# Attention in a two-layer streaming encoder: turned weights two blocks later, second exponentials left in PSUM, gates and loads cut up, sums of squares in one product

## The chip, the core and the metric

The kernel runs on one NeuronCore of a Trainium2 chip. The metric is the device time of one execution in microseconds (us). PE is the tensor engine (TensorE), DVE the vector engine (VectorE), ACT the scalar engine (ScalarE), POOL GpSimd, SP the queue that issues every DMA here.

## The reference, cut to the part that matters

Two layers of an encoder work on 1024 prompt tokens and 32 sample tokens. Branch B of each layer is differential attention: 8 heads, each with two maps of 64 dimensions, whose softmaxes are subtracted.

```python
def diff_attn_core(q, k, v, lam, mask):
    s = jnp.einsum('bhqmd,bhkmd->bhmqk', q, k).astype(jnp.float32) * (D_QK ** -0.5)
    if mask is not None:
        s = jnp.where(mask, s, -jnp.inf)
    a = jax.nn.softmax(s, axis=-1)
    a = a[:, :, 0] - lam * a[:, :, 1]
    return jnp.einsum('bhqk,bhkv->bhqv', a.astype(v.dtype), v)
...
    o_b = rmsnorm(o_b.transpose(0, 2, 1, 3), p['diff_norm_w']) * (1.0 - lam_init)
    o_b = (o_b * jax.nn.silu(z_b.reshape(B, T, H_B, DV_B))).reshape(B, T, W_B)
```

The prompt's mask is block-causal in chunks of 64 keys; a sample token sees 128 cached keys and the 32 new ones.

## The kernel before

Data are float32. The large products split a matrix into two float32r parts, high and low (`qh` and `ql`, `vh` and `vl`, `aT[..][0]` and `aT[..][1]`), so one of them is two or three matmuls; small ones are plain float32.

A layer has a stage of projections and of the other branch, then `attn` (L963), then the output projections. The order of PE's instructions in `attn` is written out by hand: the program's order is PE's order. On the other engines and on SP's queue a planner orders the instructions by its model of time. What stands under `urgent()` (L216) counts as 150 instructions earlier there.

`attn` walks over 8 heads and, in each, over nine query blocks: 8 (the samples, 32 rows) and 0 to 7 (128 rows each; block i sees (i + 1) * 128 keys). For a block, `soft` (L988) issues the scores of both maps into PSUM tiles `psc` (pool `pb`, two buffers of 1024 columns): blocks 8 and 0 to 3 put both maps into one buffer, blocks 4 to 7 take one buffer per map. DVE masks 64 columns (L1011, L1017) and takes the maxima `nm` (L1012, L1018), ACT takes the exponentials into two SBUF tiles `e` with their sums, and `combine` (L893) adds on DVE: `e[0] += c * e[1]`, with c from the sums.

After a block's scores PE runs filler (`pad`, L206): matmuls of other projections of the layer (tiles `pd`), as many as are due by the planner's prices `P_SOFT`, `P_KEY` and `P_LATE`; `share` spreads the filler over the heads so that `P_REST` is left. Then `flush` (L977) runs what is due, with filler after each:

- `turn` (L1024) transposes the block before's e on PE into `pta` (pool `pt`, two buffers of 512 columns), four key blocks to a tile; ACT casts them to the high part of `aT`, DVE subtracts for the low part. The aT tiles are taken when an even block is met (L1075), and POOL clears the part that the even query block never fills (L1077).
- `av` (L1037), after each odd block: 3 * nkb matmuls of 256 columns into `pav`.
- `attn_out` (L1102): ACT squares and copies `pav`; DVE adds the two halves of the squares (`sqb`), ACT casts the sum to float32r (`sqx`), DVE subtracts for its low part; the column sums follow two flushes later as float32r matmuls with ones (`pss`, L1120).
- `attn_row` (L1130), once per head: the norm's factors, transposed and stored to `rrow`.
- `gate_b` (L1180), in the same step: three groups of columns; for each, loads of z, o and the broadcast factors r, the product with r on POOL (L1191), the product with z on DVE (L1192), a store. All tiles come from a pool of four buffers.

Loads and casts of the heads stand together: `prep_q` (L927) for the second half of the queries after block 8, `prep_v` (L948) after block 0, `prep_k` (L912) of the next head after block 4, `prep_q` of its first half after block 5. Each issues its DMAs (into `raw`, two buffers) and at once the casts on DVE or ACT and the subtractions on POOL. The tiles `k0`, `k1` have two buffers, the q and v tiles one.

Of the kernel before, what the change touches and what calls it, by code (L numbers as in the profile page):

```python
# [20 lines left out]
TP = 1024  # L21
TS = 32
# [16 lines left out]
class Net:  # L39
    AHEAD = 150  # L40
    CUT = 26
    LATE, P_REST, P_START = 27, 23e3, 1e3
# [850 lines left out]
    def combine(s, pool, e, sums, rows, n):  # L893

        c = pool.tile([128, 1], F32, tag="cf", name="cf")
        s.nc.vector.reciprocal(c[:rows], sums[:rows, 1:2])
        s.stt(c[:rows], c[:rows], s.nlam[:rows], sums[:rows, 0:1], OP.mult, OP.mult)
        s.stt(e[0][:rows, 0:n], e[1][:rows, 0:n], c[:rows], e[0][:rows, 0:n], OP.mult, OP.add)
# [13 lines left out]
    def prep_k(s, l, pool, hd, ckt):  # L912

        raw = pool.tile([128, T], F32, tag="raw", name="kraw")
        s.ld.dma_start(out=raw, in_=s.kscr[l][2 * hd:2 * hd + 2].rearrange("m d t -> (m d) t"))
        K = []
# [10 lines left out]
    def prep_q(s, l, pool, hd, part):  # L927

        c0, w = (128, 640) if part == 0 else (0, 512)
        Q = []  # L930
        for m in range(2):
            hm = 2 * hd + m
            raw = pool.tile([128, T], F32, tag="raw", name="qraw")[:, 0:w]
            for u in range(2):
                r = slice(64 * u, 64 * u + 64)
                if part == 0:
                    s.ld.dma_start(out=raw[r, 0:TS], in_=s.qscr[l][hm, :, TP:T])
                s.ld.dma_start(out=raw[r, c0:w], in_=s.qscr[l][hm, :, part * 512:part * 512 + 512])
            if part == 0:
                s.nc.gpsimd.memset(raw[:, TS:128], 0.0)  # L940
            q = pool.tile([128, w], F32R, tag=f"q{part}{m}", name="qh")
            low = pool.tile([128, w], F32R, tag=f"ql{part}{m}", name="ql")
# [5 lines left out]
    def prep_v(s, l, pool, hd):  # L948
        vr = pool.tile([128, T], F32, tag="raw", name="vr")[:, 0:TP].rearrange("p (b f) -> p b f", b=8)
        s.ld.dma_start(out=vr, in_=s.io["v_prompt"][l, 0, hd].rearrange("(b t) f -> t b f", t=128))  # L950
        vh = pool.tile([128, 8, 128], F32R, tag="vh", name="vh")
# [11 lines left out]
    def attn(s, l, pool):  # L963
# [24 lines left out]
        def soft(hd, i, K, Q):  # L988
            rows, n, lo = (128, (i + 1) * 128, 0) if i < 8 else (TS, 160, 32)
            qc = 0 if i == 8 else (i + 1) * 128 if i < 4 else (i - 4) * 128  # L990
            e, sums = [pool.tile([128, 1024], F32, tag="e", name="e") for m in range(2)], s.s0[:, :, i, hd]
# [14 lines left out]
            else:  # L1006
                for m in range(2):
# [5 lines left out]
                    s.act(e[m][:, 0:n], p[:, 0:n], AF.Exp, bias=nm[:, m:m + 1], accum_out=sums[:, m:m + 1])  # L1013
            if pair:
# [44 lines left out]
        K, QA, turns = s.prep_k(l, pool, 0, ckt), s.prep_q(l, pool, 0, 0), []  # L1059
        s.pad(s.P_FIRST)  # L1060
        for hd in range(H):
# [4 lines left out]
            for i in (8, 0, 1, 2, 3, 4, 5, 6, 7):  # L1066
                with s.urgent():
                    e = soft(hd, i, K, QA if i in (8, 0, 1, 2, 3) else QB)
                pad(s.P_SOFT + s.P_KEY * (2 if i == 8 else i + 1) + (s.P_START if hd == 0 and i in (8, 0) else 0))
                flush(turns)  # L1070
                turns = []
                if i % 2 == 0 and i < 8:
                    j = i // 2
                    nkb = 2 * j + 2
                    aT = [[pool.tile([128, 4, 256], F32R, tag=f"aT{a}", name=f"aT{a}") for a in range(2)] for _ in range((nkb + 3) // 4)]  # L1075
# [21 lines left out]
        while late or turns:  # L1097
            s.pad(s.P_END)
            flush(turns)
            turns = []  # L1100

    def attn_out(s, l, pool, hd, po, t0, n):  # L1102
# [6 lines left out]
        if n > 128:  # L1109

            x = pool.tile([128, 256], F32R, tag="sqx", name="sqx")
            s.tt(sq[0:64], sq[0:64], sq[64:128], OP.add)
            s.cp(x[0:64], sq[0:64])
            s.tt(x[64:128], sq[0:64], x[0:64].bitcast(F32), OP.subtract)

        def rest():
            ps = s.pt.tile([128, 512], F32, tag="pt", name="pss")
            if n > 128:
                for c in range(2):
                    s.mm(ps[:, c * 2:c * 2 + 2], x[:, c * 128:c * 128 + 128], s.onesr)  # L1120
                c0 = t0 // 128
                s.cp(s.sso[:, c0:c0 + 2, hd], ps[:, 0:4:2])
# [5 lines left out]
        return (lambda: rest) if n > 128 else rest  # L1128

    def attn_row(s, l, pool, hd):  # L1130
# [8 lines left out]
        def rest():  # L1139
# [5 lines left out]
            if hd < H - 1:  # L1145
                s.gate_b(l, s.gbp, hd)
# [33 lines left out]
    def gate_b(s, l, pool, hd, groups=(0, 1, 2), act=None):  # L1180

        for g in groups:
            t0, n = GROUPS[g]
            z, o, r = (pool.tile([128, 384], F32, tag="eb" if act else "gb", name=nm) for nm in ("ez", "eo", "er"))
            s.ld.dma_start(out=z[:, :n], in_=s.zscr[l][1][hd][:, t0:t0 + n])
            s.ld.dma_start(out=o[:, :n], in_=s.obscr[l][hd][:, t0:t0 + n])
            c0, cn = t0 // 128, min(n, TP - t0) // 128
            s.ld.dma_start(out=r[:, 0:cn * 128].rearrange("p (c t) -> p c t", t=128), in_=s.rrow[l][hd][c0:c0 + cn].partition_broadcast(128))
            if g == 2:
                s.ld.dma_start(out=r[:, 256:n], in_=s.rrow[l][hd][8, 0:TS].partition_broadcast(128))  # L1190
            s.tt(o[:, :n], o[:, :n], r[:, :n], OP.mult, eng=None if act else s.nc.gpsimd)  # L1191
            s.stt(o[:, :n], o[:, :n], s.dnw[:, l:l + 1], z[:, :n], OP.mult, OP.mult)  # L1192
            if act:
                s.split(act, hd, g, o, hd % 2)
            else:
                s.st.dma_start(out=s.obscr[l][hd][:, t0:t0 + n], in_=o[:, :n])
# [323 lines left out]
```

## Time and profile before

| | |
|---|---|
| median of 3 runs | 3691.12 us (3687.35 to 3693.28) |
| the profiled execution's own time | 3680.13 us |
| its span, first to last instruction | 3678.4 us |
| busy: PE, DVE, ACT, POOL | 3368.0, 2256.4, 1520.9, 1366.3 us |
| attention of layer 0 and of layer 1 | from about 1083 to 1680 us and from 2858 to 3450 us of the span |

"Busy" counts the time in which an engine executes at least one instruction. [...] A row of waits has the idle time of an engine in front of an instruction and the instruction that ended it; "pta L76 <- DVE aT L54" is a transposition that waited for DVE's subtraction. A matmul and its weight load (PEld) are two rows; a plain float32 product is two matmul instructions.

### The profile page before, as it was taken

How to read it: one execution, taken by the hardware profiler on the slowest of the kernel's cores; microseconds unless marked ns; L12 is line 12 of the kernel's file. 1: busy time of each engine (PE TensorE's matmuls, PEld its weight loads, DVE VectorE, ACT ScalarE, POOL GpSimd, SP SyncE). 2: the span in 40 equal slices, each digit the busy share in tenths (PEclk: the TensorE clock that was granted, in tenths of full speed). 3: DMA queues.
4: the chain of work that ended last, by engine and by line, in shares of the span. 5: the costliest groups of instructions: out<-in, count | busy, mean ns of one | idle time of the engine just before them, and what ended most of it. 6: DMA issues, size and time to landing. Idle time of an engine off the chain costs nothing. (4 is left out here: it accounts for less than half of the span.)

```text
span 3678.4 us, 58386 instructions
## 1 busy us (share of the span) xinstructions
PE 3368.0 (92%) x20752; PEld 3136.4 (85%) x20752; DVE 2256.4 (61%) x3810; ACT 1520.9 (41%) x4246; POOL 1366.3 (37%) x1259
## 2 busy tenths in 40 slices
PE   8988897899999989899999999879999999889999
PEld 6888897778988888899888888878898889878997
DVE  4676758851426667865447676787143566777554
ACT  4565552123534444443244656311254344444321
POOL 2455548811134343423012223792112444343310
PEclk9999999999999999999999999999999999999999
DMA  5454534266753444556433443424775434445644
GB/s 178 116 144 142 147 117 127 85 165 197 230 147 108 129 124 133 158 150 193 138 130 94 118 119 117 134 78 131 191 233 166 130 112 132 134 149 149 177 151 151
DMA packets 618987, 526.67 MB, mean 143 GB/s; under 512 B 107028, under 2 KB 567448, under 8 KB 618312
## 3 DMA queue, kind: packets, MB, share of 16 engines
q1 hardware_dynamic: 618696, 522.94, 48.3%
q8 instruction: 164, 2.69, 0.3%
q14 instruction: 127, 1.04, 0.1%
HBM read 342.49 MB, written 180.31 MB: 142 GB/s over the span
## 5 line engine op out<-in xcount | busy, mean ns | idle before, releaser
L72 PE MATMUL pd<-h,whi 128*128 128x384 f32 (+1 forms) x2688 | 707.9, 339 | 20.3 <-ACT u L69 13.2
L72 PE MATMUL pd<-mg,whi 128*128 128x384 f32 (+1 forms) x2688 | 698.1, 336 | 13.5 <-ACT u L69 11.7
L54 POOL TENSOR_TENSOR wlo<-wraw,whi 128x512 fp32r<-128x512 f32 (+1 forms) x220 | 432.7, 1976 | 494.6 <-ACT whi L69 444.0
L72 PEld LDWEIGHTS pd<-h,whi 128*128 128x128 f32 x2688 | 479.2, 195 | 29.8 <-ACT u L69 14.5
L72 PEld LDWEIGHTS pd<-mg,whi 128*128 128x128 f32 x2688 | 474.7, 193 | 22.1 <-ACT u L69 12.5
L72 PE MATMUL pd<-h,wlo 128*128 128x384 f32 (+1 forms) x1344 | 451.2, 336 | 0.0
L72 PE MATMUL pd<-mg,wlo 128*128 128x384 f32 (+1 forms) x1344 | 449.1, 334 | 0.0
L69 ACT CAST whi<-wraw 128x1024 fp32r<-128x1024 f32 (+1 forms) x304 | 259.1, 865 | 192.0 <-PE pd L72 61.7
L66 ACT ACTIVATE e<-psc,nm 32x160 f32<-32x160 f32 (+8 forms) x288 | 200.8, 700 | 307.3 <-DVE nm L1012 152.5
L72 PEld LDWEIGHTS pd<-h,wlo 128*128 128x128 f32 x1344 | 261.0, 194 | 2.3 <-issue 1.2
L72 PEld LDWEIGHTS pd<-mg,wlo 128*128 128x128 f32 x1344 | 259.0, 193 | 2.5 <-issue 1.2
L72 PE MATMUL ptok<-whi,mg 128*128 128x512 f32 x768 | 241.2, 395 | 5.2 <-DVE rt L54 3.4
L63 DVE SCALAR_TENSOR_TENSOR acc<-u,convT,acc 128x1059 f32<-128x1059 f32 x144 | 218.9, 1523 | 2.7
L72 PE MATMUL pr<-mg,whi 128*128 128x384 f32 (+1 forms) x768 | 196.2, 339 | 15.7 <-DVE rt L54 15.7
L72 PE MATMUL pr<-h,whi 128*128 128x384 f32 (+1 forms) x768 | 194.2, 338 | 15.3 <-DVE rt L54 15.2
L72 PE MATMUL pd<-oa,whi 128*128 128x384 f32 (+1 forms) x768 | 193.8, 330 | 5.2 <-DVE egt L63 3.7
L72 PE MATMUL pd<-ob,whi 128*128 128x384 f32 (+1 forms) x768 | 184.4, 326 | 5.7 <-ACT whi L69 2.0
L54 DVE TENSOR_TENSOR wlo<-wraw,whi 128x1024 fp32r<-128x1024 f32 x84 | 107.7, 1283 | 120.9 <-ACT whi L69 119.2
L72 PEld LDWEIGHTS ptok<-whi,mg 128*128 128x128 f32 x768 | 144.3, 189 | 37.3 <-DVE rt L54 3.6
L76 PE MATMUL pta<-ident,e 128*128 128x128 f32 (+1 forms) x608 | 98.4, 288 | 74.3 <-DVE aT L54 53.8
L54 DVE TENSOR_TENSOR itmp<-ub,X 128x624 f32<-128x624 f32 (+56 forms) x188 | 152.1, 809 | 15.1 <-DMA ub<-ublks 6.3
L72 PEld LDWEIGHTS pr<-mg,whi 128*128 128x128 f32 x768 | 140.2, 198 | 19.9 <-DVE rt L54 19.1
(319 smaller groups left out, 8043.1 us busy)
## 6 DMA issues: line engine op xcount, KB each, us to landing
wraw<-in_w_in SPq DMA_DIRECT2D x160, 512.0 KB
srec<-grec SPq DMA_DIRECT2D x128, 384.0 KB
grec<-rec SPq DMA_DIRECT2D x128, 192.0 KB
z<-zo SPq DMA_DIRECT2D x96, 192.0 KB
wraw<-in_w_ada SPq DMA_DIRECT2D x64, 256.0 KB
qraw<-qscr SPq DMA_DIRECT2D x128, 128.0 KB
egt<-z SPq DMA_DIRECT2D x64, 192.0 KB
eo<-ob SPq DMA_DIRECT2D x60, 192.0 KB
```

What stands on the lines that cost most here:

```text
L54: (eng or s.nc.vector).tensor_tensor(out, a, b, op=op)
L63: s.nc.vector.scalar_tensor_tensor(out, a, sc, b, op0=op0, op1=op1)
L66: s.nc.scalar.activation(out, a, func, **kw)
L69: s.nc.scalar.copy(out, a)
L72: s.nc.tensor.matmul(out, lhsT, rhs, start=start, stop=stop)
L76: s.nc.tensor.transpose(out, a, s.ident[0:n, 0:n])
```

## The change

- `combine` reads the second map's exponentials from PSUM: ACT writes them over the scores they come from. Only one `e` tile per block is taken. The combine is issued after the block's filler.
- `flush` runs the turns of the block before the last (`ready`), so a block is turned two blocks behind its scores. The aT tiles are taken in `turn`; POOL's clearing goes.
- In `av` the last key block is multiplied with the odd query block's 128 columns only, right after the first product.
- Loads and casts are separate functions; each load stands one or two blocks ahead of its casts, and the next head's first q half is cast after block 6.
- The sums of squares are plain float32 matmuls of `sq` with a column of ones, one flush earlier.
- The gates of a head are issued one group at a time, loads in one flush and use in the next; DVE's product with z comes first, POOL's with r second. Outside `attn` the same function serves the last head.
- `LATE`, the number of late steps that the filler's spread counts per head, is 29, not 27.

```diff
-    LATE, P_REST, P_START = 27, 23e3, 1e3
+    LATE, P_REST, P_START = 29, 23e3, 1e3
...
-        s.stt(e[0][:rows, 0:n], e[1][:rows, 0:n], c[:rows], e[0][:rows, 0:n], OP.mult, OP.add)
+        s.stt(e[0][:rows, 0:n], e[1], c[:rows], e[0][:rows, 0:n], OP.mult, OP.add)
...
-            e, sums = [pool.tile([128, 1024], F32, tag="e", name="e") for m in range(2)], s.s0[:, :, i, hd]
+            e, sums = [pool.tile([128, 1024], F32, tag="e", name="e"), None], s.s0[:, :, i, hd]
...
-                    s.act(e[m][:, 0:n], p[:, 0:n], AF.Exp, bias=nm[:, m:m + 1], accum_out=sums[:, m:m + 1])
+                    to = p if m else e[0]
+                    s.act(to[:, 0:n], p[:, 0:n], AF.Exp, bias=nm[:, m:m + 1], accum_out=sums[:, m:m + 1])
+                e[1] = p[:, 0:n]
...
-                for m in range(2):
-                    s.act(e[m][:rows, 0:n], pv[:rows, m, lo:lo + n], AF.Exp, bias=nm[:rows, m:m + 1], accum_out=sums[:rows, m:m + 1])
-            s.combine(pool, e, sums, rows, n)
-            return e[0]
+                e[1] = pv[:rows, 1, lo:lo + n]
+                for m, to in enumerate((e[0][:rows, 0:n], e[1])):
+                    s.act(to, pv[:rows, m, lo:lo + n], AF.Exp, bias=nm[:rows, m:m + 1], accum_out=sums[:rows, m:m + 1])
+            return e[0], lambda: s.combine(pool, e, sums, rows, n)
...
         def turn(hd, i, e, aT, v):
+            if i % 2 == 0:
+                aT[:] = [[pool.tile([128, 4, 256], F32R, tag=f"aT{a}", name=f"aT{a}") for a in range(2)] for _ in range((i + 5) // 4)]
...
-            s.accumulate(po[:, 0:256], [(v[:, kb], aT[kb // 4][a][:, kb % 4])
-                                        for kb in range(nkb) for v, a in ((vh, 0), (vl, 0), (vh, 1))])
+            order = [(0, 0)] + [(nkb - 1, x) for x in range(3)] + [(kb, x) for kb in range(nkb - 1) for x in range(3) if kb or x]
+            for k, (kb, x) in enumerate(order):
+                q0 = 128 if kb == nkb - 1 else 0
+                s.mm(po[:, q0:256], (vh, vl, vh)[x][:, kb], aT[kb // 4][x // 2][:, kb % 4, q0:256], start=k == 0, stop=k == len(order) - 1)
...
-                    e = soft(hd, i, K, QA if i in (8, 0, 1, 2, 3) else QB)
+                    e, comb = soft(hd, i, K, QA if i in (8, 0, 1, 2, 3) else QB)
                 pad(s.P_SOFT + s.P_KEY * (2 if i == 8 else i + 1) + (s.P_START if hd == 0 and i in (8, 0) else 0))
-                flush(turns)
-                turns = []
+                with s.urgent():
+                    comb()
+
+                flush(ready)
+                ready, turns = turns, []
                 if i % 2 == 0 and i < 8:
...
-                    for a in range(2):
-                        nc.gpsimd.memset(aT[(nkb - 1) // 4][a][:, (nkb - 1) % 4, 0:128].bitcast(F32), 0.0)
+                    aT = []
                 if i == 8:
                     turns.append(lambda hd=hd, e=e, vs=vs: sample(hd, e, vs))
-                    QB = s.prep_q(l, pool, hd, 1)
+                    raws = s.load_q(l, pool, hd, 1)
...
                 if i == 0:
-                    v.extend(s.prep_v(l, pool, hd))
+                    QB = s.prep_q(pool, raws, 1)
+                if i == 1:
+                    raws = s.load_v(l, pool, hd)
+                if i == 2:
+                    v.extend(s.prep_v(pool, raws))
                 if hd < H - 1:
...
+                    if i == 2:
+                        raws = s.load_k(l, pool, hd + 1)
                     if i == 4:
-                        Kn = s.prep_k(l, pool, hd + 1, ckt)
-                    if i == 5:
-                        QA = s.prep_q(l, pool, hd + 1, 0)
+                        Kn = s.prep_k(pool, raws, ckt)
+                        raws = s.load_q(l, pool, hd + 1, 0)
+                    if i == 6:
+                        QA = s.prep_q(pool, raws, 0)
...
-        while late or turns:
+        while late or turns or ready:
             s.pad(s.P_END)
-            flush(turns)
-            turns = []
+            flush(ready)
+            ready, turns = turns, []
...
-        if n > 128:
-
-            x = pool.tile([128, 256], F32R, tag="sqx", name="sqx")
-            s.tt(sq[0:64], sq[0:64], sq[64:128], OP.add)
-            s.cp(x[0:64], sq[0:64])
-            s.tt(x[64:128], sq[0:64], x[0:64].bitcast(F32), OP.subtract)
...
-                    s.mm(ps[:, c * 2:c * 2 + 2], x[:, c * 128:c * 128 + 128], s.onesr)
+                    s.mm(ps[:, c:c + 1], sq[:, c * 128:c * 128 + 128], s.ones[:, 0:1])
                 c0 = t0 // 128
-                s.cp(s.sso[:, c0:c0 + 2, hd], ps[:, 0:4:2])
+                s.cp(s.sso[:, c0:c0 + 2, hd], ps[:, 0:2])
...
-        return (lambda: rest) if n > 128 else rest
+        return rest
...
-                s.gate_b(l, s.gbp, hd)
+                return lambda: gate(0)
+
+        def gate(g):
+
+            x = s.gate_load(l, s.gbp, "gb", hd, g)
+
+            def use():
+                s.gate_use(l, hd, g, *x)
+                if g < 2:
+                    return lambda: gate(g + 1)
+            return use
...
+    def gate_use(s, l, hd, g, z, o, r, act=None):
+        t0, n = GROUPS[g]
+        s.stt(o[:, :n], o[:, :n], s.dnw[:, l:l + 1], z[:, :n], OP.mult, OP.mult)
+        s.tt(o[:, :n], o[:, :n], r[:, :n], OP.mult, eng=None if act else s.nc.gpsimd)
```

## Rows read from the trace of the kernel before

**Rows 1.** Windows of both attention stages: us, busy per engine, clock, DMA share, GB/s.
```profile
1083.00:1680.00 597.00, 545.59 (x3446) 519.95 (x3445) 407.79 (x742) 266.47 (x715) 242.57 (x216) 0.97 0.46 135
2858.00:3450.00 592.00, 540.63 (x3404) 514.64 (x3403) 406.36 (x736) 265.48 (x711) 238.42 (x214) 0.96 0.45 133
```

**Rows 2.** Windows of seven stretches at the low clock: their sum.
```profile
sum 47.60, PE 28.30 PEld 27.52 DVE 39.06 ACT 25.68 POOL 31.66; mean PE 4.04 PEld 3.93 DVE 5.58 ACT 3.67 POOL 4.52
```

**Rows 3.** PE's waits in both stages: us, times, longest us; layer 0, then 1.
```profile
PE pta L76 <- DVE aT L54: 25.4, 8, 6.3
PE psc L72 <- ACT e L66: 6.8, 5, 2.0
PE pta L76 <- DVE e L63: 3.7, 2, 1.9
...
PE pta L76 <- DVE aT L54: 28.5, 8, 6.8
PE pta L76 <- DVE e L63: 4.2, 2, 2.8
```

**Rows 4.** Timeline at a change of heads: start us, us, engine, what [idle <-releaser].
```profile
1228.99 1.44 DVE L920 CAST k<-kraw 64x1056 fp32r<-64x1056 f32 x2 [2.04 <-DMA kraw<-kscr]
1229.83 5.42 POOL L54 TENSOR_TENSOR k<-kraw,k 64x1056 fp32r<-64x1056 f32 x2 [4.88 <-DVE k L920]
1230.46 2.52 DVE L54 TENSOR_TENSOR sqb<-sqb 64x256 f32<-64x256 f32 x1
1233.01 0.40 ACT L69 CAST sqx<-sqb 64x256 fp32r<-64x256 f32 x1 [6.84 <-DVE sqb L54]
1233.45 2.09 DVE L54 TENSOR_TENSOR sqx<-sqb,sqx 64x256 fp32r<-64x256 f32 x1 [0.47 <-ACT sqx L69]
1235.57 1.16 DVE L54 TENSOR_TENSOR aT<-pta,aT 128x512 fp32r<-128x512 f32 x2
1236.31 0.90 PE L76 MATMUL pta<-ident,e 128*128 128x128 f32 x3 [6.30 <-DVE aT L54]
```

**Rows 5.** DVE's groups by shape, layer 0's attention: busy us, mean ns, idle before.
```profile
L54 DVE TENSOR_TENSOR sqx<-sqb,sqx 64x256 fp32r<-64x256 f32 x32 | 30.3, 946 | 4.5 <-ACT sqx L69 3.8
L54 DVE TENSOR_TENSOR sqb<-sqb 64x256 f32<-64x256 f32 x32 | 28.9, 902 | 22.4 <-ACT sqb L66 21.8
L63 DVE SCALAR_TENSOR_TENSOR zo<-zt,pd 128x384 f32<-128x384 f32 x16 | 8.7, 546 | 1.0 <-ACT zt L66 1.0
L63 DVE SCALAR_TENSOR_TENSOR e<-e,cf 128x384 f32<-128x384 f32 x8 | 4.9, 618 | 0.2
```

**Rows 6.** Timeline, PE: a float32 product, products of 256 columns, transposes.
```profile
1008.86 0.39 PE L72 MATMUL po<-w,srec 128*128 128x128 f32 x2
1204.83 0.28 PE L72 MATMUL pav<-aT,vh 128*128 128x256 f32 x1
1205.06 0.41 PE L72 MATMUL pav<-aT,vh 128*128 128x256 f32 x2
1214.12 0.82 PE L76 MATMUL pta<-ident,e 128*128 128x128 f32 x6
```

**Rows 7.** Timeline: block 6's combine and the next second map's scores; heads 1, 2.
```profile
1147.47 1.15 DVE L63 SCALAR_TENSOR_TENSOR e<-e,cf 128x896 f32<-128x896 f32 x1
1150.45 0.39 PE L72 MATMUL psc<-k,qh 128*128 128x512 f32 x1
1217.02 0.50 PE L72 MATMUL psc<-k,qh 128*128 128x512 f32 x1
1218.37 1.15 DVE L63 SCALAR_TENSOR_TENSOR e<-e,cf 128x896 f32<-128x896 f32 x1
```

**Rows 8.** DVE's waits in layer 0's attention.
```profile
DVE eo L63 <- POOL eo L54: 48.1, 20, 4.7
```

**Rows 9.** Windows of the second and third head of layer 0.
```profile
1160.40:1227.20 66.80, 64.12 (x421) 61.08 (x420) 42.67 (x81) 31.97 (x87) 27.10 (x26) 1.00 0.42 123
1227.20:1298.60 71.40, 65.06 (x416) 62.54 (x415) 45.30 (x83) 33.47 (x90) 30.36 (x27) 0.95 0.40 118
```

More of the change, by code (lines that the diff above doesn't have):

```diff
@@ L910, in attn_cache, with load_k, prep_k @@
         return ckt, rest
-    def prep_k(s, l, pool, hd, ckt):
+    def load_k(s, l, pool, hd):
         raw = pool.tile([128, T], F32, tag="raw", name="kraw")
         s.ld.dma_start(out=raw, in_=s.kscr[l][2 * hd:2 * hd + 2].rearrange("m d t -> (m d) t"))
+        return raw
+    def prep_k(s, pool, raw, ckt):
         K = []
@@ L925, in prep_k, with load_q @@
         return K
-    def prep_q(s, l, pool, hd, part):
+    def load_q(s, l, pool, hd, part):
         c0, w = (128, 640) if part == 0 else (0, 512)
-        Q = []
+        raws = []
         for m in range(2):
@@ L940, in prep_q @@
                 s.nc.gpsimd.memset(raw[:, TS:128], 0.0)
-            q = pool.tile([128, w], F32R, tag=f"q{part}{m}", name="qh")
-            low = pool.tile([128, w], F32R, tag=f"ql{part}{m}", name="ql")
+            raws.append(raw)
+        return raws
+    def prep_q(s, pool, raws, part):
+        Q = []
+        for m, raw in enumerate(raws):
+            q = pool.tile(list(raw.shape), F32R, tag=f"q{part}{m}", name="qh")
+            low = pool.tile(list(raw.shape), F32R, tag=f"ql{part}{m}", name="ql")
             s.nc.vector.tensor_copy(q, raw)
@@ L946, in prep_q, with load_v, prep_v @@
         return Q
-    def prep_v(s, l, pool, hd):
+    def load_v(s, l, pool, hd):
         vr = pool.tile([128, T], F32, tag="raw", name="vr")[:, 0:TP].rearrange("p (b f) -> p b f", b=8)
         s.ld.dma_start(out=vr, in_=s.io["v_prompt"][l, 0, hd].rearrange("(b t) f -> t b f", t=128))
+        return vr
+    def prep_v(s, pool, vr):
         vh = pool.tile([128, 8, 128], F32R, tag="vh", name="vh")
@@ L1057, in sample @@
             return rest
-        K, QA, turns = s.prep_k(l, pool, 0, ckt), s.prep_q(l, pool, 0, 0), []
+        K = s.prep_k(pool, s.load_k(l, pool, 0), ckt)
+        QA = s.prep_q(pool, s.load_q(l, pool, 0, 0), 0)
+        turns, ready = [], []
         s.pad(s.P_FIRST)
@@ L1067, in attn @@
                 with s.urgent():
-                    e = soft(hd, i, K, QA if i in (8, 0, 1, 2, 3) else QB)
+                    e, comb = soft(hd, i, K, QA if i in (8, 0, 1, 2, 3) else QB)
                 pad(s.P_SOFT + s.P_KEY * (2 if i == 8 else i + 1) + (s.P_START if hd == 0 and i in (8, 0) else 0))
-                flush(turns)
-                turns = []
+                with s.urgent():
+                    comb()
+                flush(ready)
+                ready, turns = turns, []
                 if i % 2 == 0 and i < 8:
-                    j = i // 2
-                    nkb = 2 * j + 2
-                    aT = [[pool.tile([128, 4, 256], F32R, tag=f"aT{a}", name=f"aT{a}") for a in range(2)] for _ in range((nkb + 3) // 4)]
-                    for a in range(2):
-                        nc.gpsimd.memset(aT[(nkb - 1) // 4][a][:, (nkb - 1) % 4, 0:128].bitcast(F32), 0.0)
+                    aT = []
                 if i == 8:
                     turns.append(lambda hd=hd, e=e, vs=vs: sample(hd, e, vs))
-                    QB = s.prep_q(l, pool, hd, 1)
+                    raws = s.load_q(l, pool, hd, 1)
                 else:
@@ L1182, in gate_b, with gate_load @@
         for g in groups:
[L1183 to L1196, printed above, removed]
+            s.gate_use(l, hd, g, *s.gate_load(l, pool, "eb" if act else "gb", hd, g), act)
+    def gate_load(s, l, pool, tag, hd, g):
+        t0, n = GROUPS[g]
+        z, o, r = (pool.tile([128, 384], F32, tag=tag, name=nm) for nm in ("ez", "eo", "er"))
+        s.ld.dma_start(out=z[:, :n], in_=s.zscr[l][1][hd][:, t0:t0 + n])
+        s.ld.dma_start(out=o[:, :n], in_=s.obscr[l][hd][:, t0:t0 + n])
+        c0, cn = t0 // 128, min(n, TP - t0) // 128
+        s.ld.dma_start(out=r[:, 0:cn * 128].rearrange("p (c t) -> p c t", t=128), in_=s.rrow[l][hd][c0:c0 + cn].partition_broadcast(128))
+        if g == 2:
+            s.ld.dma_start(out=r[:, 256:n], in_=s.rrow[l][hd][8, 0:TS].partition_broadcast(128))
+        return z, o, r
+    def gate_use(s, l, hd, g, z, o, r, act=None):
+        t0, n = GROUPS[g]
+        s.stt(o[:, :n], o[:, :n], s.dnw[:, l:l + 1], z[:, :n], OP.mult, OP.mult)
+        s.tt(o[:, :n], o[:, :n], r[:, :n], OP.mult, eng=None if act else s.nc.gpsimd)
+        if act:
+            s.split(act, hd, g, o, hd % 2)
+        else:
+            s.st.dma_start(out=s.obscr[l][hd][:, t0:t0 + n], in_=o[:, :n])
     def gated(s, l, pool, tag, act, branch, hd, g):
```

## The prediction

> **What bounds the kernel now.** I read the windows of the two attention stages first, then the waits of their stretches, then the timeline around one of the long waits, and last the groups by shape for prices.
>
> TensorE (PE) runs one hand-written order, and it is nearly always busy: 545.59 of 597 us in layer 0's attention and 540.63 of 592 in layer 1's [rows 1]. ScalarE (ACT) and GpSimd (POOL) are busy less than half of that time and VectorE (DVE) about 70% of it. So these stages end when PE has worked off its order, and what can be won there is PE's idle time, 51.4 + 51.4 = 102.8 us, and what the clock loses behind it. [...]
>
> Over half of the idle time has one cause: transposes (pta) that wait for the DVE subtraction into aT, 25.4 us in 8 waits and 28.5 in 8 [rows 3]. Transposes of an e that was not combined yet cost 3.7 + 4.2 us, and scores that wait for an exponential 6.8 us in layer 0 (I take layer 1 alike, 13.6 in all) [rows 3]. The rest is 102.8 - 53.9 - 7.9 - 13.6 = 27 us of small ones.
>
> The 6.30 us wait at 1236.31 shows the mechanism [rows 4]. At the change of heads DVE waits 2.04 us for kraw, casts k for 1.44 us, then stands 2.52 us in the folding add sqb while POOL runs its two k subtractions (5.42 us). ACT has sat 6.84 us in front of the sqx cast, with the aT casts queued behind it; DVE's sqx subtraction takes 2.09 us more; only then, at 1235.57, come the aT subtractions that free the transposes' PSUM tile.
>
> **The change, part by part.**
>
> *Plain sums of squares.* Two DVE operations and one ACT cast per pair of blocks go. DVE spent 28.9 + 30.3 us on them in layer 0 [rows 5], so some 118 us in both layers, off PE's path except at the change of heads. There, in rows 4, aT could start when the k casts end, at 1230.43, in place of 1235.57: 5.1 of the 6.30 us go, and 1.2 stay (kraw and k are still in front). At that ratio 53.9 us shrink to 10. PE pays for it: a product of plain f32 runs as two instructions that start 0.11 us apart (0.39 - 0.28) [rows 6], so each sum takes four weight loads where two stood: 2 x 0.11 x 64 sums = +14 us. It lies on PE's order with nothing to hide it.
>
> *av's last key block at 128 columns.* 3 x 4 x 8 x 2 = 192 products lose half their columns. Two products of 256 columns start 0.13 us apart (0.41 - 0.28), and six transposes of 128 columns 0.11 us apart ((0.82 - 0.28) / 5) [rows 6]: the weight load sets the pace of the short ones. I take 0.01 us each, -2 us; the bounds are 0 and 0.02 (-4). [...] The aT memsets on POOL also go; POOL is not the bound, and it only runs ahead better.
>
> *Turning two blocks behind.* PE's transposes of a block come one block later, so e is always there: the 7.9 us go. The PSUM tiles of the transposes are as many as before, so for the aT wait the delay alone changes nothing. At the end the last head's chain runs as many flushes as before, beside the filler that is kept for it.
>
> *Second exponentials in PSUM.* ACT writes the same columns. DVE's combine now has one PSUM operand. The nearest pair of rows: 384 columns with a PSUM operand take 546 ns, the combine of 384 from SBUF 618 [rows 5], so I count 0, with bounds of -0.07 and +0.07 us per block, on DVE. [...]
> The new wait is what matters: the PSUM of the second map is held until the combine ends, not until the exponential ends. The second map's scores of the next block (blocks 4 to 7) take that buffer, and behind them in PE's order stands everything else: filler products, transposes, av. In the first head the combine of block 6 ended at 1148.62 (1147.47 + 1.15) and the scores that would wait started at 1150.45, 1.8 us later; in the second head it ended at 1219.52, and they had started at 1217.02, 2.5 us too early [rows 7].
>
> *Gates spread, DVE first.* What makes the combine late in that second head is the gate: DVE waits for POOL's product 48.1 us in a layer, in 20 waits [rows 8], and POOL for the broadcast of rrow. The first head has no gate in front of it. The change puts DVE's step first, so it waits for two loads, not for POOL; the same DMAs go out on SP's queue (three or four per group), one group per two flushes. I count this as what keeps the new wait near zero: the scores' 13.6 us stay as they are. If the loads are late, combines, reductions and aT steps queue behind DVE's gate step.
>
> *Loads spread.* Each load is issued one or two blocks ahead of its casts; the number of DMAs and casts stays. They pass each other on SP's queue, in the same order. But the k and q tiles come free when the old head's scores are done, whatever the place in the code, so I count nothing for it. Bounds: -10 us (the 2.04 us for kraw in rows 4 at 14 changes of heads, if a third shows on PE) and as much the other way (the next head's q, cast one block later, comes late to its first scores, with POOL's 5.42 us for k in front of its subtractions).
>
> *The rest at nothing.* `LATE` only spreads the same filler; the sums and the head's factors come a flush earlier and nobody waits for them; after the stage the last head's gate swaps two DVE products.
>
> **The sum**, against the profiled execution (3680.1 us, span 3678.4): aT waits -44, e waits -8, of the small 27 us -12 (ACT and DVE have less queued), clock -20 of 25, PE's products +14 - 2: -72 us, so 3608 us. The shown median, 3691.1, is 11 us (0.3%) above the profiled execution; on it the forecast is **3619 us**. A check: a head with a 2.5 us wait took 66.80 us at full clock, the next, with the 6.30 us wait, 71.40 at 0.95 [rows 9]; 4.6 us x 16 heads = 74.
>
> **Rivals.**
>
> *A: the burst stays.* Tile releases, not code places, put the q and k casts and POOL's subtractions at the change of heads; another DVE step slides in where sqb stood. For: in rows 4 DVE waits for a load and POOL blocks 5.4 us whoever comes next. Against: sqb and sqx are the two steps in front of aT. Then half of the aT waits goes: -27 - 8, clock -10, products +12: -33, 3658 us.
>
> *B: the combine holds PE (slower).* Place: second map's scores of blocks 4 to 7, 8 heads, 2 layers, 64 blocks. The combine is now issued after the block's filler, so DVE's casts and aT steps can come before it, and it ends when the next scores are due. For: the 2.5 us in rows 7, and scores that already wait for exponentials. Against: 1.8 us to spare where no gate stands. The gain of 72 us is used up at 72 / 64 = 1.1 us per block; from there it is slower. At 1.7 us per block: 109 - 72 = +37, 3728 us.
> [...]
>
> *C: nearly all goes.* With e, aT and gate waits gone, the small stalls and the clock follow: -103 - 25 + 12 = -116, 3575 us. Against: filler that waits for DVE and ACT is untouched.
>
> **How the numbers follow.** Forecast 0.55, A 0.20, C 0.11, B 0.14. About 0.2% (7 us) is what a measurement of this kernel can tell from no change. Forecast and C are faster, A too in nine of ten cases with the rest within 0.2%, B slower but for 0.02 within: faster 0.55 + 0.11 + 0.18 = 0.84, same 0.04, slower 0.12. The range runs from 3570, just below C, to 3690, which takes in A and its bounds; B and what lies below C are left out.
>
> **What would show it.** No sqb and sqx on DVE or ACT, pta waiting for aT under 10 us per layer, no wait of over 4 us at a change of heads; clock 0.98 or more in both stretches; 256 weight loads of pss with 128 columns. DVE's gate step should wait for a DMA, not for POOL. The forecast is wrong if psc waits for the combine's e or cf on DVE by more than some 20 us per layer (B), or if aT's waits stay over 10 us per layer with k casts in front (A).

## The result, and the profile after

The changed kernel takes 3645.69 us in the median (3642.68 to 3652.91, 4 runs), the kernel before 3690.28 beside it (3687.35 to 3693.28, 4 runs): a ratio of 0.9883, 95% interval 0.9867 to 0.9899, so 1.2% faster. The forecast was 3619 us, 72 us less than before; 44.6 came. The profiled executions, which the sum was made against, differ by 37.1 us (3680.13 and 3643.02). That difference is the one taken apart below. The other 7.5 us come of the profiled executions being 10.2 and 2.7 us faster than their medians.

The windows of both attention stages, from 14 us before a stage's first scores or transposes to 4 us behind the last (columns as in [rows 1]; by these bounds the first window there would end at 1674, with the same idle time):

```profile
1079.00:1653.00 574.00, 540.10 (x3480) 517.70 (x3479) 362.47 (x675) 259.97 (x680) 231.68 (x155) 0.98 0.47 139
2838.00:3415.00 577.00, 544.01 (x3492) 521.49 (x3492) 365.08 (x675) 260.96 (x680) 232.25 (x155) 0.98 0.47 139
```

PE idles 33.9 + 33.0 = 66.9 us where it idled 102.8 [rows 1]: 35.9 us less, nearly the whole difference. The column of the clock is a share of full speed. The clock's records in both traces are 1.00 or 0.50, nothing between, and the seven stretches of [rows 2] are at 0.50 throughout. So PE spent 2 x 0.02 x 1151 = 46 us at the low clock, where [rows 1] give 2 x 0.03 x 597 + 2 x 0.04 x 592 = 83. It works at about half the pace there: in the changed kernel scores of 384 columns start 0.31 us apart at 0.50 (1406.33 and 1406.64) and 0.17 us apart at 1.00 (1399.90 and 1400.07). With the busy share of [rows 2], 28.30 of 47.60 us, the 37 us less take an estimated 11 us off PE's busy time (to within a few us, the clock having two digits), and the longer order of products gives about as much back: over the whole span PE is busy 3366.1 us, before 3368.0. PE's waits of the two stages (us, times, longest us; layer 0, then 1):

```profile
PE psc L72 <- DVE e L63: 15.5, 8, 4.9
PE pta L76 <- ACT oTb L69: 8.6, 7, 3.1
PE pav L72 <- DVE aT L54: 5.7, 5, 2.0
PE pta L76 <- ACT sso L69: 3.9, 5, 1.6
...
PE psc L72 <- DVE e L63: 13.8, 8, 4.7
PE pta L76 <- ACT sso L69: 7.5, 5, 4.3
PE pta L76 <- ACT oTb L69: 7.1, 5, 3.1
PE pav L72 <- DVE aT L54: 4.5, 4, 2.2
```

Of the waits in [rows 3] the 53.9 us for aT and the 7.9 for e are gone, and some 14 us of small ones too (for zo and egt, which DVE makes of the filler's results, and for ckt, the cached keys). Three others stand in their place: scores (psc) that wait for the combine, 29.3 us, where 13.6 were spent on waits for the exponential; transposes that wait for ACT's copies out of pav and pss (oTb and sso), 27.1 us; av that waits for aT, 10.2 us. Before, the second and third stood at 8.9 and 2.4 us:

```profile
PE pta L76 <- ACT oTb L69: 2.9, 1, 2.9
PE pta L76 <- ACT sso L69: 1.2, 1, 1.2
...
PE pta L76 <- ACT oTb L69: 2.5, 1, 2.5
PE pta L76 <- ACT sso L69: 2.3, 2, 1.5
```

Some 77 us went and 41.7 came, so the net is less than half of what was removed.

The longest of the new waits (timeline of DVE, POOL and PE: start us, us, engine, what, idle before it and releaser):

```profile
1396.01 0.62 DVE L63 SCALAR_TENSOR_TENSOR eo<-eo,dnw,ez 128x384 f32<-128x384 f32 x1 [1.09 <-DMA eo<-ob]
...
1400.91 2.34 POOL L54 TENSOR_TENSOR wlo<-wraw,whi 128x1024 fp32r<-128x1024 f32 x1
1401.12 2.45 DVE L63 SCALAR_TENSOR_TENSOR eo<-eo,dnw,ez 128x288 f32<-128x288 f32 x1 [3.62 <-DMA eo<-ob]
...
1404.18 1.01 DVE L63 SCALAR_TENSOR_TENSOR e<-psc,cf,e 128x768 f32<-128x768 f32 x1
...
1405.34 0.77 PE L72 MATMUL psc<-k,qh 128*128 128x512 f32 x1 [4.93 <-DVE e L63]
```

DVE's gate step waits 3.62 us for a load, then takes 2.45 us beside POOL's wlo (0.62 us at 1396.01, alone and with more columns). Block 5's combine is queued behind it, and PE's second map of block 6 behind the combine. In both stages DVE waits in this way for 77 us, where it waited for POOL before [rows 8]:

```profile
DVE eo L63 <- DMA eo<-ob: 37.9, 17, 3.8
...
DVE eo L63 <- DMA eo<-ob: 39.4, 19, 3.6
```

A change of heads, to be read against [rows 4]:

```profile
1218.69 0.71 DVE L923 CAST k<-kraw 64x1056 fp32r<-64x1056 f32 x1
1218.79 5.46 POOL L54 TENSOR_TENSOR k<-kraw,k 64x1056 fp32r<-64x1056 f32 x2 [6.32 <-DVE k L923]
...
1219.61 2.11 DVE L63 SCALAR_TENSOR_TENSOR cf<-cf,nlam,s 32x1 f32<-32x1 f32 x1
...
1222.06 1.13 DVE L54 TENSOR_TENSOR aT<-pta,aT 128x512 fp32r<-128x512 f32 x2
```

The k casts and POOL's 5.46 us stand where they stood. A one-column step of the combine now holds DVE for 2.11 us, where sqb did for 2.52, but it is one such step, not two with an ACT cast between them, and aT follows 0.34 us behind it.

### The profile page after: what moved, and what is told of

Same layout as the page of the kernel before. It is cut to its first block, busy times and chain, and to the rows that moved or that the text cites. A ratio compares the mean times of both kernels' runs of the same rounds, so it can differ in the third digit from the quotient of the medians.

```text
span 3641.2 us, 58240 instructions
## 1 busy us (share of the span) xinstructions
PE 3366.1 (92%) x20880; PEld 3142.2 (86%) x20880; DVE 2170.1 (60%) x3682; ACT 1509.9 (41%) x4182; POOL 1343.5 (37%) x1131
## 4 chain that ended last, share of the span: by engine, by line
PE 37%; DMA 7%; DVE 5%; POOL 4%; issue 3%; ACT 2%; SPq 0%; DVEq 0%; POOLq 0%; ACTq 0%
PE pd L72 20%; PE ptok L72 7%; DMA Gb<-grow 2%; PE pav L72 2%; PE psc L72 2%; DMA eo<-ob 2%; PE pr L72 1%; PE pts L72 1%; POOL X L54 1%; PE pta L76 1%; POOL itmp L54 1%; PE po L72 1%; POOL ro L54 1%; POOL wlo L54 1%; DMA kraw<-kscr 1%
## 5 line engine op out<-in xcount | busy, mean ns | idle before, releaser
L72 PEld LDWEIGHTS pd<-h,whi 128*128 128x128 f32 x2688 | 476.0, 193 | 24.8 <-ACT u L69 14.4
L66 ACT ACTIVATE e<-psc,nm 32x160 f32<-32x160 f32 (+2 forms) x144 | 101.1, 702 | 327.1 <-DVE nm L1025 185.8
L72 PE MATMUL pr<-mg,whi 128*128 128x384 f32 (+1 forms) x768 | 196.6, 339 | 15.7 <-DVE rt L54 15.7
L72 PE MATMUL pr<-h,whi 128*128 128x384 f32 (+1 forms) x768 | 194.7, 339 | 13.6 <-DVE rt L54 13.6
L72 PE MATMUL pd<-ob,whi 128*128 128x384 f32 (+1 forms) x768 | 186.5, 327 | 10.2 <-ACT ob L69 8.5
L72 PE MATMUL psc<-k,qh 128*128 128x512 f32 (+3 forms) x416 | 142.9, 351 | 29.5 <-DVE e L63 29.3
L54 DVE TENSOR_TENSOR itmp<-ub,X 128x624 f32<-128x624 f32 (+56 forms) x188 | 152.2, 810 | 15.7 <-DMA ub<-ublks 6.2
```

The lines of the kernel that those rows point to most:

```text
L54: (eng or s.nc.vector).tensor_tensor(out, a, b, op=op)
L66: s.nc.scalar.activation(out, a, func, **kw)
L72: s.nc.tensor.matmul(out, lhsT, rhs, start=start, stop=stop)
```

## The experiments

PE's idle time below is that of both attention stages, window less PE busy, from the same view and the same bounds as above. It is that of one execution each, and the windows do not hold the same amount of filler, so a few us of it decide nothing. All ratios are against the kernel before, run beside. In each section the two or three readings of the kernel that the runs were to tell apart have names (theory S, rival D and so on), which the expectation explains.

| kernel | ratio | 95% interval | PE idle, us |
|---|---|---|---|
| the change | 0.9883 | 0.9867 to 0.9899 | 66.9 |
| sums_only | 0.9904 | 0.9890 to 0.9917 | 78.1 |
| sums_back | 1.0045 | 1.0032 to 1.0057 | 102.0 |
| gates_wait | 0.9868 | 0.9853 to 0.9884 | 57.5 |
| e_sbuf | 0.9859 | 0.9846 to 0.9873 | 59.8 |
| one_behind | 0.9882 | 0.9864 to 0.9900 | 68.6 |
| loads_back | 0.9870 | 0.9850 to 0.9890 | 62.8 |
| gates_old | 0.9873 | 0.9855 to 0.9891 | 77.8 |
| high_first | 0.9864 | 0.9844 to 0.9884 | 67.5 |
| k_dve | 0.9959 | 0.9945 to 0.9973 | 85.5 |
| kqv_dve | 1.0049 | 1.0033 to 1.0065 | 111.3 |
| gates_pool | 0.9846 | 0.9822 to 0.9870 | 51.4 |
| gates_k | 0.9823 | 0.9807 to 0.9839 | 49.8 |

**sums_only.** The kernel before with the plain sums alone:

```diff
-            x = pool.tile([128, 256], F32R, tag="sqx", name="sqx")
-            s.tt(sq[0:64], sq[0:64], sq[64:128], OP.add)
-            s.cp(x[0:64], sq[0:64])
-            s.tt(x[64:128], sq[0:64], x[0:64].bitcast(F32), OP.subtract)
...
-                    s.mm(ps[:, c * 2:c * 2 + 2], x[:, c * 128:c * 128 + 128], s.onesr)
+                    s.mm(ps[:, c:c + 1], sq[:, c * 128:c * 128 + 128], s.ones[:, 0:1])
...
```

> The kernel before with nothing but the plain sums of squares (no sqb, sqx on DVE and ACT, one flush earlier). Theory S (the folded sums are what the transposes' tile waited for): pta waiting for DVE's aT falls from 53.9 us to under 20 in both stages, and with 14 us more on PE and some 10 from the clock the time is 25 to 45 us less, 0.988 to 0.993 of before. Rival D (it is the later turning and the spread loads and gates that freed the aT step): aT's waits stay above 40 us and the time lies at 0.997 to 1.004, since the sums cost PE 14 us.

0.9904: some 35 of the 45 us. The wait for aT all but vanishes (53.9 to 1.8 us), and at once another one stands there, PE's waits in layer 0 and 1:

```profile
PE pta L76 <- ACT oTb L69: 19.0, 6, 4.3
...
PE pta L76 <- ACT oTb L69: 16.6, 6, 4.0
```

35.6 us, where 5.4 were before. Theory S holds for the cause of the aT waits (its edit also puts the sums one flush earlier; the two are not told apart). Of the 52.1 us that the aT waits lose, 30.2 come back as waits for ACT's copy out of pav, the next user of the same two PSUM tiles; PE's idle time falls by 24.7 us.

**sums_back.** The changed kernel with the lines above turned round, the sums two flushes later.

> The changed kernel with the folded sums put back (two additions on DVE, a cast on ACT, float32r products two flushes later). Theory S: the aT waits come back with over 25 us in both stages, 0.993 to 0.999 of before. Rival D: the other parts keep the aT step in time, its waits stay under 10 us, and PE gets its 14 us back: 0.983 to 0.988.

1.0045, slower than the kernel before. Not pta but pss now is the first to want that tile, PE's waits of both stages:

```profile
PE pss L72 <- DVE aT L54: 24.2, 6, 6.6
PE psc L72 <- DVE e L63: 11.6, 8, 3.8
...
PE pss L72 <- DVE aT L54: 25.0, 5, 6.3
PE psc L72 <- DVE e L63: 10.9, 8, 4.3
```

The aT lateness is back in full (49.2 us there, 10.0 more at pta), the waits for the combine come on top (22.5 us), and the mean clock is 0.95 in both stages (0.97 and 0.96 in [rows 1]). So theory S stands, with something that neither side had expected (both had put this run below the kernel before): without the plain sums the other parts cost 0.45%; with them they are worth 0.2% (0.9904 to 0.9883, with intervals that overlap). The gain is that of the sums.

**gates_wait** and **e_sbuf**, two ways to take away the waits for the combine. Six gate buffers and one flush more between load and use:

```diff
-            return use
+            return lambda: use
...
-                    s.gbp = pool(st, f"gb{l}", 4)
+                    s.gbp = pool(st, f"gb{l}", 6)
```

> The changed kernel with six gate buffers in place of four and the use of a gate group one flush further behind its loads. Theory G (what is left of the stalls comes from DVE's gate step, which waits for its load with the combines, the maxima and the aT steps queued behind it, 77 us of DVE idle in both stages): that idle time falls under 20 us, PE's waits for the combine from 29.3 to under 15, those for oTb and sso from 27.1 to under 20, the time to 0.978 to 0.985 of before. Rival P (it is the hold on PSUM itself, with the combine behind the filler): the waits for the combine stay above 22 us, 0.986 to 0.990.

And the second exponentials of blocks 8 and 0 to 5 in SBUF (one of the edited lines):

```diff
...
-                    to = p if m else e[0]
+                    to = p if m and i > 5 else e[m]
...
```

> The changed kernel with the second map's exponentials of blocks 8 and 0 to 5 in an SBUF tile again, so that only blocks 6 and 7 hold PSUM until their combine. Theory G: PE's waits for the combine (29.3 us) fall under 8, but scores wait for the exponentials instead by some 10 us, and the gate step's delay shows on at aT, oTb and sso; 5 to 15 us less than the changed kernel, 0.984 to 0.987 of before. Rival P: most of the 29.3 us and the clock behind them come back: 0.978 to 0.983.

In gates_wait DVE's wait for the gate's load halves, 77.3 to 40.4 us, and PE's waits for oTb and sso shrink from 27.1 to 6.4; but those for the combine stay (30.4 us) and av waits 18.5 us for aT instead of 10.2. Rival P has the combine's waits and the time right (0.9868); theory G has only the shrinking waits for oTb and sso, though PE's idle time falls by 9.4 us. In e_sbuf the waits for the combine are gone (0.6 us for the exponential remain), so holding PSUM is what makes them; but 29.3 us of waits removed bring 7.1 us of idle time. Its longest two waits in layer 0:

```profile
PE pta L76 <- ACT oTb L69: 9.0, 7, 2.0
PE pav L72 <- DVE aT L54: 6.2, 5, 2.0
```

Theory G's time for e_sbuf holds (0.9859), P's does not; the 10 us of waits for exponentials that G had named did not come. Either way most of the wait moves on: what PE no longer waits for at one product it waits for at others, further on.

**one_behind**, **loads_back**, **gates_old**: each undoes one part in the changed kernel.

```diff
...
-                flush(ready)
-                ready, turns = turns, []
+                flush(turns)
+                turns = []
...
```

> The changed kernel with the turns one block behind the scores, as before, and the load and cast of v one block earlier so that the first av still has it. Theory T (two blocks matter only because a block's e is then surely combined): transposes wait for e again by 5 to 15 us in both stages, 0.989 to 0.993 of before. Rival U (the combine now stands behind the filler, so one block is far too short): over 30 us of waits for e, above 0.996. Third: nothing to see, 0.986 to 0.989.

```diff
...
-                        Kn = s.prep_k(pool, raws, ckt)
-                        raws = s.load_q(l, pool, hd + 1, 0)
-                    if i == 6:
-                        QA = s.prep_q(pool, raws, 0)
+                        Kn = s.prep_k(pool, s.load_k(l, pool, hd + 1), ckt)
+                    if i == 5:
+                        QA = s.prep_q(pool, s.load_q(l, pool, hd + 1, 0), 0)
```

> The changed kernel with every load of q, k and v issued right before its casts again, at the places of before. Theory N (tile releases, not code places, set these steps; counted at nothing in the forecast): 0.986 to 0.991 of before, PE's idle time within 10 us of the changed kernel's 66.6 in both stages. Rival L (the spread loads keep DVE from standing in front of a DMA): PE idle over 85 us, 0.993 or more.

```diff
-                return lambda: gate(0)
+                s.gate_b(l, s.gbp, hd)
...
-        s.stt(o[:, :n], o[:, :n], s.dnw[:, l:l + 1], z[:, :n], OP.mult, OP.mult)
         s.tt(o[:, :n], o[:, :n], r[:, :n], OP.mult, eng=None if act else s.nc.gpsimd)
+        s.stt(o[:, :n], o[:, :n], s.dnw[:, l:l + 1], z[:, :n], OP.mult, OP.mult)
```

> The changed kernel with a head's gate in one piece again, POOL's product first. Theory G (DVE's wait in the gate step is what the combine and the aT steps queue behind): DVE waits for POOL's product by some 90 us instead of 77 for a load, in a burst at one place; PE's waits for the combine grow from 29.3 to over 40 us, 0.991 to 0.997 of before. Rival (the spreading is worth nothing): waits for the combine 22 to 36 us, 0.986 to 0.990.

All three lie on the changed kernel's time. With turns one block behind the transposes wait for e by 4.7 us; by its time it is the third case. The loads were worth nothing, as counted (N). The gates in one piece leave the waits for the combine at 29.7 us, layer 0 and 1:

```profile
PE psc L72 <- DVE e L63: 15.1, 10, 2.4
...
PE psc L72 <- DVE e L63: 14.6, 10, 2.8
```

So the spreading did not keep them low, and theory G's burst is not seen there: waits and time are the rival's. PE idles 10.9 us more, but its windows hold 81 PE instructions fewer and are only 3 us longer.

**high_first.** On e_sbuf, av's products with the high part first, and pav copied before it is squared:

```diff
-        s.act(sq[:, :n], po[:, 0:n], AF.Square)
         s.cp(o[:, :n], po[:, 0:n])
+        s.act(sq[:, :n], o[:, :n], AF.Square)
...
+            order += [(nkb - 1, 2)] + [(kb, 2) for kb in range(nkb - 1)]
```

> The kernel of e_sbuf with two further edits: in av all products with the high part of aT come before those with the low part, and attn_out copies pav first and squares the copy, so that PSUM comes free one ACT step earlier. Theory A (what is left of PE's stalls is a chain of short waits, each of which ends on its own): pav waiting for aT falls from 10.7 to under 4 us, pta waiting for oTb from 20.1 to under 15, 0.981 to 0.985 of before. Rival B (DVE and ACT are late as a whole, and PE only waits a little further on): idle time of PE stays within 5 us of 59, 0.985 to 0.988.

Waits for aT rise from 10.7 to 14.9 us, for oTb they stay (20.1 and 19.8), idle time is 67.5 us where e_sbuf has 59.8: these reorderings, on PE and on ACT, buy nothing. The time is rival B's, though its bound of 5 us around 59 is passed.

**k_dve** and **kqv_dve** ask whether POOL makes DVE late, by moving POOL's subtractions to DVE:

```diff
-            s.tt(k[b, 0:T], raw[a], k[a, 0:T].bitcast(F32), OP.subtract, eng=s.nc.gpsimd)
+            s.tt(k[b, 0:T], raw[a], k[a, 0:T].bitcast(F32), OP.subtract)
```

(and the same for k's cached part; in kqv_dve for q and v too)

> The changed kernel with the subtractions of k (64 x 1056 and 64 x 128) on DVE in place of POOL. Theory L (beside POOL's long subtractions DVE's operations on SBUF stretch: the one-column cf took 1.33 and 2.02 us there against 0.22 elsewhere, so POOL makes DVE late): the long cf go, PE's idle time in both stages falls from 66.6 to under 55 us, 0.979 to 0.985 of before. Rival O (DVE is late by its own order and load): the k steps only lengthen its queue, idle 62 us or more, 0.986 to 0.993.

> The changed kernel with the subtractions of k, q and v all on DVE. Theory L: PE's idle time falls under 45 us, 0.975 to 0.982 of before. Rival O: DVE gets some 45 us of work more in each layer, idle time 66 to 90 us, 0.987 to 0.998.

Theory L's forecast falls: both are slower, and by more than rival O had said. The long one-column steps do go in k_dve (the group that averages 1248 ns in the changed kernel's layer 0 averages 204), and PE's idle time rises all the same. The windows of k_dve:

```profile
1083.00:1677.00 594.00, 549.50 (x3487) 525.74 (x3486) 371.48 (x708) 260.31 (x680) 182.00 (x123) 0.97 0.46 134
2865.00:3455.00 590.00, 549.00 (x3489) 526.21 (x3488) 370.48 (x707) 260.64 (x680) 182.14 (x123) 0.96 0.46 135
```

DVE is busy only 14.4 us more than in the changed kernel (741.97 and 727.55) and POOL 99.8 less, yet PE idles 18.6 us more. The place of the new steps tells more than their length, as k_dve's timeline at the first head shows:

```profile
1105.18 2.10 DVE L923 CAST k<-kraw 64x1056 fp32r<-64x1056 f32 x2 [4.95 <-DMA kraw<-kscr]
1107.32 1.25 DVE L54 TENSOR_TENSOR k<-kraw,k 64x1056 fp32r<-64x1056 f32 x1
...
1108.78 1.25 DVE L54 TENSOR_TENSOR k<-kraw,k 64x1056 fp32r<-64x1056 f32 x1
...
1110.38 0.30 DVE L63 SCALAR_TENSOR_TENSOR e<-psc,cf,e 32x160 f32<-32x160 f32 x1
...
1110.83 0.55 PE L72 MATMUL psc<-k,qh 128*128 128x256 f32 x1 [7.19 <-DVE e L63]
```

Block 8's combine is queued behind the next head's k, for which DVE first waits 4.95 us. PE pays 7.19 us, and 7.9 at the same place in layer 1; in the changed kernel the same two waits are 1.97 and 2.12. That makes 11 of the 18.6 us.

**gates_pool.** DVE out of the gates:

```diff
-        s.cp(o[:, :n], po[:, 0:n])
+        s.act(o[:, :n], po[:, 0:n], AF.Copy, scale=s.dnw[:, l:l + 1])
...
-        s.stt(o[:, :n], o[:, :n], s.dnw[:, l:l + 1], z[:, :n], OP.mult, OP.mult)
+        s.tt(o[:, :n], o[:, :n], z[:, :n], OP.mult, eng=None if act else s.nc.gpsimd)
```

> The changed kernel with DVE taken out of the gates: ACT scales o by dnw while it copies it from PSUM, and both products run on POOL. DVE loses 38 us of work in 42 steps and the 77 us in which it stood in front of the gate's load. Theory G (that stand is what makes the combine, the maxima and the aT steps late): PE's idle time in both stages falls from 66.6 to under 50 us, 0.978 to 0.984 of before. Rival O (DVE is late at the changes of heads, where k and q are cast, and the gate only stands there by turns): idle time 58 to 70 us, 0.985 to 0.990.

0.9846 lies between the two forecasts (theory G up to 0.984, rival O from 0.985) and its interval reaches into both; the idle time, 51.4 us, is much nearer to G's bound of 50 than to O's 58. Against the changed kernel the intervals overlap. Its windows:

```profile
1085.00:1651.00 566.00, 540.56 (x3483) 519.92 (x3482) 350.11 (x655) 266.09 (x680) 251.08 (x176) 0.98 0.49 141
2836.00:3405.00 569.00, 543.08 (x3489) 522.36 (x3488) 351.81 (x653) 266.13 (x680) 250.50 (x176) 0.98 0.48 141
```

POOL is 37.7 us busier in both together and DVE 25.6 less; the waits for the combine fall to 15.7 us, for oTb and sso to 10.4, and av's for aT rise to 21.6:

```profile
PE psc L72 <- DVE e L63: 7.3, 6, 2.5
...
PE psc L72 <- DVE e L63: 8.4, 6, 2.8
```

The longest wait, 5.3 us for the aT of 1429.00, again has a wait of DVE for a load in front of it:

```profile
1425.06 1.44 DVE L923 CAST k<-kraw 64x1056 fp32r<-64x1056 f32 x2 [3.93 <-DMA kraw<-kscr]
1426.53 2.55 DVE L54 TENSOR_TENSOR zo<-zo,zoa 128x288 f32<-128x288 f32 x1
1429.00 1.01 DVE L54 TENSOR_TENSOR aT<-pta,aT 128x512 fp32r<-128x512 f32 x2
```

**gates_k.** gates_pool with the k casts on ACT:

```diff
-            s.nc.vector.tensor_copy(k[a, 0:T], raw[a])
+            s.cp(k[a, 0:T], raw[a])
```

> The kernel of gates_pool with one more edit: the casts of k to float32r run on ACT in place of DVE, 1.44 us less on DVE at each change of heads. Theory O (what is left comes from DVE's burst at the changes of heads, where the k casts stand): PE's idle time in both stages falls from 51 to under 42 us, 0.978 to 0.983 of before. Rival R (ACT, which then casts k in front of its exponentials and copies, is late in DVE's place): waits for oTb and sso grow over 20 us, idle 48 us or more, 0.984 to 0.990.

0.9823 [0.9807, 0.9839]: 3628.83 us, faster than both the kernel before and the changed one (whose interval begins at 0.9867). Its idle time, 49.8 us, is gates_pool's, and its waits for oTb and sso do not grow (8.5 us): the time falls as theory O has it, the idle time stays as R has it, and neither reason is borne out. Against gates_pool the intervals overlap, so what the k casts are worth stays open.

## Why the prediction was right, and where it was off

**Faster, and inside the range: right.** The step that carried the forecast was the plain sums of squares in front of aT. The aT waits went whole (53.9 us against the 44 counted), sums_only has them at 1.8 us and gives 35 of the 45 us, and sums_back brings the aT lateness back. Rival A (the burst stays, half of the aT waits goes) named something true, the k casts and POOL's 5.46 us are where they were, but drew the wrong price from it. Nor did POOL's subtractions block whatever came next: beside them DVE's reciprocal took 0.15 us (1219.43) and two aT subtractions 1.13 (1222.06), and only the step into cf, at 2.11 us, was long. In size it came nearer all the same: its sum was -33 us, the forecast's -72, and 37.1 were measured. That is chance, since none of the aT waits that A kept are there. And the range was wide enough, from 3570 to 3690, to hold either; being inside it says little for the sum.

**e waits -8 and small ones -12: right in size.** 7.9 us of waits for e and some 14 for zo, egt and ckt are gone. In one_behind 4.7 us of the first come back, and the kernel's time does not move.

**PE's products +14 - 2: right by the rows.** Plain float32 sums show four instructions where two stood, 288 weight loads of pss in all, 256 of them of 128 columns, and the profile counts 128 PE instructions more. PE's timeline has narrow av products 0.11 us apart and those of 256 columns 0.12; the prediction's rows had 0.11 and 0.13. The weight loads there start 0.11 us apart, too (1229.73, 1229.84 and 1229.95), and those of pss, whose products have one column, 0.12 ((0.54 - 0.19) / 3, four loads from 1224.08). That the load sets the pace of the short ones, as the prediction has it, fits these rows; no run varied the load alone. The rows:

```profile
1218.74 0.28 PE L72 MATMUL pav<-aT,vl 128*128 128x256 f32 x1
1218.86 0.40 PE L72 MATMUL pav<-aT,vh 128*128 128x256 f32 x2
...
1224.20 0.50 PE L72 MATMUL pss<-ones,sqb 128*128 128x1 f32 x4
...
1229.79 0.27 PE L72 MATMUL pav<-aT,vl 128*128 128x128 f32 x1
1229.90 0.27 PE L72 MATMUL pav<-aT,vh 128*128 128x128 f32 x1
```

**The combine from PSUM at nothing: right.** 384 columns take 614 ns, against 618 from SBUF [rows 5]:

```profile
L63 DVE SCALAR_TENSOR_TENSOR e<-psc,cf,e 128x384 f32<-128x384 f32 x8 | 4.9, 614 | 0.2
```

**"I count this as what keeps the new wait near zero": the step that failed.** The 13.6 us of the scores, which were to stay as they are, became 29.3. The sentence behind it, that combines queue behind DVE's gate step if its load is late, is what the trace shows at 1401. But the gate was no guard against it: with the gates of before (gates_old) the same wait is 29.7 us. DVE waited 91.8 us for POOL's product in the kernel before and 77.3 us for the load in the changed one; the step changed what it waits for, not whether. And 7.5 of the 29.3 us stand in the stages' first heads, where no gate is in front. With DVE out of the gate (gates_pool) the waits for the combine halve; they go only where PSUM is not held (e_sbuf).

**Rival B was half right.** The combine does hold PE, with 15.5 and 13.8 us below the 20 us per layer that would have decided for it. Its place was too narrow: the 7.5 us of the first heads stand at blocks 0 to 3, which hold both maps in one buffer. Its price was wrong in kind: it took each us of wait for a us of time. Where PSUM is not held (e_sbuf), 29.3 us of waits less are 7.1 us of idle time less.

**Not named at all, and the larger miss: what is late next behind aT.** The 44 us were entered as if nothing else wanted the same two PSUM tiles; alone (sums_only) the 52.1 us of aT waits that went were worth 24.7 us of idle time. The check by heads (4.6 us x 16 = 74) made the same mistake, since it too counted the whole length of a wait as gained. In the changed kernel, with the aT subtraction early, transposes waited for ACT's copies out of pav and pss, 8.9 us before, 27.1 after, and av for aT, 2.4 and 10.2. With the combine's 15.7 us more that makes 41.7 us of new waits. Set against the 77 us that went, 35.9 are left on PE.

**Clock -20 of 25: mis-sized.** No run shows the 25 us. The windows show 83 us at the low clock before and 46 after, from which the 11 us above are estimated. Of 102.8 us of idle time 66.9 stayed. So the sum, against the profiled execution: idle time -36, clock -11, products +12: -35, and 37.1 were measured. The last two are not measured apart; together they are the -1.9 us of PE's busy time over the whole span.

**The signs.** No folding steps into sqb and sqx, no pta waiting for aT, 256 wide weight loads of pss, a clock of 0.98 in both stages and DVE's gate step waiting for a DMA: these came as written. One sign did not, that no wait of over 4 us is left at a change of heads: 4.29 us of wait for sso stand at the end of a head in layer 1 (ACT idle for 4.02 us in front of an exponential, because DVE's gate step had taken 1.83 us of waiting and 2.81 of work).

**What stays open** is which of DVE's waits the idle time that is left comes from (66.9 us in the changed kernel, 49.8 in the best version). DVE idles for over 400 us of the two stages in every version of the changed kernel (423 in the changed one, window less busy), mostly in front of ACT's exponentials, its aT casts and the gate's load, and the order in which it meets them is the planner's. That this order is the cause is argued, not shown: no run here changed it alone.

## What to carry to other kernels

A wait removed from the engine that bounds can be worth far less than its own length (here 24.7 us for 52.1, and 7.1 for 29.3), because the next wait is close behind: before entering it in a sum, list who else takes that buffer in turn and when its other releasers are done. DVE's waits for a late DMA reached PE through what was queued behind them: 3.62 us for the gate's load at 1401.12 and 4.93 us of PE for the combine behind it, 4.95 us for kraw at k_dve's first head and 7.19 us of PE. Taking off DVE the step that waits (the gate, in gates_pool) brought PE's idle time down by 15.5 us, though the gain in time over the changed kernel is not clear of noise. Parts that are worth next to nothing beside another can cost without it (sums_back): undo each part in the finished kernel as well as adding it to the old one.

## What the runs showed of the hardware

In these traces DVE steps with two inputs in SBUF stretched beside POOL's subtractions, even the smallest: the combine's one-column factor took 2.11 us beside k's subtraction (1219.61) and 0.22 us at 1225.12. The samples' block, which stands at the change of heads, in layer 0 of the changed kernel and of k_dve, where k's subtractions are not on POOL:

```profile
L63 DVE SCALAR_TENSOR_TENSOR cf<-cf,nlam,s 32x1 f32<-32x1 f32 x8 | 10.0, 1248 | 0.2
...
L63 DVE SCALAR_TENSOR_TENSOR cf<-cf,nlam,s 32x1 f32<-32x1 f32 x8 | 1.6, 204 | 0.2
```

Much of what the folded sums cost was that, too. All their steps in the kernel before (ns: least, median, most):

```profile
L54 DVE TENSOR_TENSOR sqb<-sqb x64: 420/422/2569, 1126.7 to 3453.0; 64x256 f32<-64x256 f32 x64
L54 DVE TENSOR_TENSOR sqx<-sqb,sqx x64: 418/420/2101, 1128.1 to 3453.9; 64x256 fp32r<-64x256 f32 x64
```

By the medians 128 of them are 54 us of work; they took some 118 [rows 5]. The combine itself stretched as well before: at 1111.09, beside k's subtraction on POOL, 128 columns took 2.59 us, and 0.35 us in the next two heads. With one input in PSUM none of its 144 steps takes more than 1.29 us, and those are the ones of 1024 columns. The step of 2.11 us ends at 1221.72, just after the first of POOL's two subtractions (2.92 us from 1218.79) is over; what holds the step until then is not shown.

What the stretching costs in time is not shown. In k_dve it is gone from the samples' block, and the kernel is slower than the changed one; but k_dve puts k's steps in front of the combine at the same time.
